# Wide output projection, sample rows and first index key in column tiles, first loads in places of their own

## The chip, the cores and the metric

The kernel runs on one core of a Trainium2 chip. The metric is the time of one execution on the device in microseconds (us); lower is better. Five engines work side by side, each through its own instructions in a fixed order: PE (TensorE, matmuls; its weight loads are a row of their own, PEld), DVE (VectorE), ACT (ScalarE), POOL (GpSimd) and SP (SyncE, which issues the DMAs).

## The reference

One inference step of a layer with three groups of attention heads, for 512 prompt rows and 32 sample rows that continue a cache of 1024 rows. D is 1024; all arrays are fp32.

```python
def layer(x, ...):                      # prompt: 512 rows; sample: 32 rows with caches
    z = rmsnorm(x, norm_mix_g) @ w_in   # 1024 -> 13 column groups
    qa, ka, va, ga, qb, kb, vb, gb, qm, gm, qi, ki, wi = split(z)
    # A, 6 heads x 64: own chunk of 64 rows and 8 chunks before it, relative-position bias
    # B, 6 heads x 64: an indexer (8 heads x 32, ONE shared key ki of 32 columns) scores all
    #    earlier rows; attention only over the best 128 (prompt) or 256 (sample)
    # M, 4 heads x 64: attention to 256 memory rows, mk, mv = rmsnorm(mem) @ w_mem_kv
    mix = concat(A(...) * silu(ga), B(...) * silu(gb), M(...) * silu(gm))   # rows x 1024
    return rmsnorm(x + mix @ w_out, norm_out_g)
```

The outputs are y for prompt and sample, and the new keys, values and index keys.

## The kernel before, in words

**Arithmetic.** A product in fp32 accuracy is made of three fast matmuls in the type fp32r: each operand is split in a high part and a low remainder, and h·wh, l·wh and h·wl are summed in PSUM (`tokens`, `group_t`, `out_part`). So each chunk of weights goes through a chain: `w_load` (SP) brings `raw`, `rounded` (ACT) makes `wh`, and a subtraction (`w_split`) makes `wl`, on POOL, or on DVE for the chunks named in `WV`. The input goes the same way: ACT makes `xTh`, DVE `xTl` (512 prompt columns and 32 sample columns); `xF` is the sample part in plain fp32, made on POOL.

**Sample rows.** The 32 sample rows would fill a quarter of PE's 128 columns. In the input projections they are therefore done in plain fp32 with the unsplit `raw`, as four matmuls side by side in four tiles of 32 columns (`divided`), each with a quarter of the contraction. Elsewhere they are not in four tiles: in the attention of the sample (`sample`, with mix 0 for A, 1 for B and 2 for M) the value blocks stand still (64 columns, two tiles) and the 32 probabilities of a head move (`mix_of`); in the output projection the sample is a fifth tile of rows, `oS`, with its high and low parts as 64 columns.

**Order.** No engine decides at run time what comes next. A planner (`Line`) runs while the program is built: it keeps a clock for each engine, adds for each operation a modelled duration (`cost`), for DVE and POOL a rule on the memory port that they share (`port`), and lets generators (tasks) issue their operations when the modelled clocks say that inputs are there (`at`, `sure`). What comes out is one static list for each engine. PE's list is filled by the projections; pieces of attention are put between them when they are ready in the model. So a change in any number of the model moves operations everywhere.

**Stages on PE.** The string `START` orders the first loads. The first projection is the index one (`index_group`), by chunks of two rows of blocks, with 296 columns for tiles 1 to 3 and only the 32 key columns for tile 0. Then come the groups of `EARLY` (`ka`, `va`, `mk`, `mv`, then the transposed ones `qa`, `ga`, `qm`, `gm`) and of `LATE` (`gb0`, `kb`, `qb`, `vb`, `gb1`, `gb2`). A's and M's attention units (`attend`) are woven in from the moment that their inputs exist, then B's. The output projection has two parts in `out_part`: first the heads of A and M, in four column blocks of 256, which fills PE beside B's last units, then, when all units are done, the heads of B in two blocks of 512, each as two accumulations of 256 columns. `residual` (DVE) adds the products to x in `xr`, and `settle` makes the last norm with the running sum `ss`: ACT squares, DVE adds, POOL takes the root (`ALU.pow`), DVE and ACT scale, SP stores.

In the profile all recorded operations carry one line, L273, the call inside the planner's wrapper (L288 after the change), so instructions are told apart by tiles. `bank` is a PSUM bank, `xT` the normed and transposed input, `k`, `q` keys and queries of a unit, `z` and `pt` probabilities and their transposes, `oA`, `oB`, `oM` the gated results by group, with h and l for the parts.

Of the kernel before, what the change touches and what calls it, by code (L numbers as in the profile page):

```python
# [17 lines left out]
P = 128  # L18
# [16 lines left out]
WV = (0, 2)  # L35
# [7 lines left out]
EARLY = ("ka", "va", "mk", "mv", "qa0", "qa1", "qa2", "ga0", "ga1", "ga2", "qm0", "qm1", "gm0", "gm1")  # L43
# [3 lines left out]
class Line:  # L47
# [4 lines left out]
    def __init__(self):  # L52
        self.clk = dict.fromkeys(("PE", "DVE", "ACT", "POOL", "SP", "DMA"), 0.0)
        self.ready, self.used = {}, {}
        self.boxes = {}
        self.tables = {"exp": (AF.Exp, AF.Tanh)}
        self.table = None
        self.mode = None
        self.taken = []
        self.tasks = []  # L60
        self.seq = 0
        self.margin = 0.3
        self.time = 0.0
        self.window, self.busy, self.slow = 0.0, 0.0, True
        self.warm = None

    def cost(self, eng, op, outs, ins, kw):
        if eng == "PE":
# [12 lines left out]
            if mode != self.mode:  # L81
                self.mode = mode
                d += 0.095 + (0.104 if fast else 0.056) * mode[1] / P
            return d
# [6 lines left out]
        if eng == "ACT":  # L91
# [5 lines left out]
            return t  # L97
        return 0.15 + n * (0.0034 if op == "tensor_scalar" else 0.0021)
# [204 lines left out]
def hybrid_step(ctx: ExitStack, tc: tile.TileContext, a: dict):  # L303
# [80 lines left out]
    oS = cp.tile([P, 8, 2 * T], F32R, name="oS")  # L384
    m8 = cp.tile([P, 8], F32, name="m8")

    rs, r16, ss = (cp.tile([P, 8], F32, name=n) for n in ("rs", "r16", "ss"))
# [56 lines left out]

    w_in, w_out, w_mem = a["w_in"], a["w_out"], a["w_mem_kv"]
    NATURAL = {"i": (QI, 296), "ka": (KA, 384), "va": (VA, 384), "kb": (KB, 384), "qb": (QB, 384), "vb": (VB, 384)}
    TURNED = {"qa": QA, "ga": GA, "qm": QM, "gm": GM, "gb": GB}
    for nm in ("i",) + EARLY + LATE:
# [4 lines left out]
        elif nm in ("mk", "mv"):  # L453
            c0 = 256 * (nm == "mv")
            w_cols(w_mem, c0, c0 + 256)
# [14 lines left out]
    met = []  # L470
    allowed = [0]

    def w_load():
        party = {p + j for _, p, _ in parties for j in range(NK // 2)}
        for i, (w, k, nk, lo, hi) in enumerate(w_list):
            yield from line.wait(lambda: allowed[0] > i and (i < 8 or len(split) > i - 4 and (i - 4 not in party or i - 4 in met)))
# [5 lines left out]
            else:  # L482
                yield wp.free("raw")
                raw = wp.tile([P, nk, hi - lo], F32, tag="raw", name="raw", bufs=4)
# [3 lines left out]
    def w_split():  # L488
        at = {}
        for i in range(len(w_list)):  # L490
            far = i >= n_in + 3 and i % 2
            yield from line.wait(lambda: len(raws) > i and (not far or wq))
            pw, n = (rp, 4) if i < 4 else (wq[0], 2) if far else (wp, 3)
            mine = at.setdefault(n, [])
            yield from line.wait(lambda: len(mine) < n or used["done"] > mine[-n])
            mine.append(i)
            raw = raws[i]
            yield max(line.at(raw), pw.free("wl"))
            wh = pw.tile(list(raw.shape), F32R, tag="wh", name="wh", bufs=n)
            wl = pw.tile(list(raw.shape), F32R, tag="wl", name="wl", bufs=n)  # L500
# [56 lines left out]
    def tokens(acc, xh, xl, w, c, t, c0, c1, first, last):  # L557
# [3 lines left out]
        for kk in range(2):  # L561
            k = 2 * c + kk
# [4 lines left out]
            PE.matmul(o, h, wl[:, kk, c0:c1], start=False, stop=last and kk == 1)  # L567

    def needs_of(xh, xl, w, c, t):
        k = slice(2 * c % 4, 2 * c % 4 + 2)  # L570
        return w + tuple(x[c // 2][:, k, t * P:(t + 1) * P] for x in (xh, xl))
# [11 lines left out]
    def group_n(xh, xl, n, tiles, done, then, r0, there):  # L583
# [3 lines left out]
        for c in range(NK // 2):  # L587
            w = w_next()
            line.until(lambda: there[0] > c)
            for t in range(tiles):  # L590
                yield needs_of(xh, xl, w, c, t) + ((acc[t],) if c == 0 else ())
                tokens(acc[t], xh, xl, w, c, t, 0, n, c == 0, c == NK // 2 - 1)
                made[0] += c == NK // 2 - 1
# [32 lines left out]
    mTl = [cp.tile([P, 4, NM], F32R, tag=n, name="mTl") for n in ("kb", "gate1")]  # L626
# [3 lines left out]
    def x_load():  # L630
        c = len(x_raw)
        yield from line.wait(lambda: x_done[0] > c - 3)
        t = rp.tile([P, 2, N], F32, tag="xr", name="xr", bufs=3)
# [5 lines left out]
    def m_load():  # L639
# [3 lines left out]
        m_raw.append(t)  # L643

# [41 lines left out]
    def norms():  # L686
        for i in range(NT + 1 + NM // P):
# [7 lines left out]
            G.tensor_scalar(ss[:n, i:i + 1], ss[:n, i:i + 1], EPS, None, op0=ALU.add)  # L695
            G.tensor_tensor(rs[:n, i:i + 1], ss[:n, i:i + 1], nhalf[:n], op=ALU.pow)
            G.tensor_scalar(r16[:n, i:i + 1], rs[:n, i:i + 1], 1.0 / 16, None, op0=ALU.mult)
# [40 lines left out]
    def start():  # L738
# [12 lines left out]
        DMA.dma_start(gT[1], a["norm_mem_g"])  # L751
# [11 lines left out]
    def load_tables(d):  # L763
# [5 lines left out]
        def scale():  # L769
            for t in range(NT):  # L770
# [23 lines left out]

    rot, wI = ix.tile([P, NT, 9, 32], F32, name="rot"), ix.tile([P, NT, 8], F32, name="wI")
# [3 lines left out]
    def i_done(t, acc):  # L799
# [4 lines left out]
        if t > 0:  # L804
            A.copy(wI[:, t, :], acc[:, 288:296])
# [5 lines left out]
        if t > 0:  # L811
            for r in (rs, r16):
                G.tensor_scalar(wI[:, t, :], wI[:, t, :], r[:, t:t + 1], None, op0=ALU.mult)
        indexed.append(t)

    def index_group():
        acc = take(NT)
        for c in range(NK // 2):
            w = w_next()
            line.until(lambda: x_done[0] > c)  # L820
            for t in (1, 2, 3, 0):
                yield needs_of(xTh, xTl, w, c, t)
                tokens(acc[t], xTh, xTl, w, c, t, *((256, 288) if t == 0 else (0, 296)), c == 0, c == NK // 2 - 1)
                if c == NK // 2 - 1:
                    line.spawn(i_done(t, acc[t]))

# [173 lines left out]
    bi = {n: cp.tile([P, 1], I32, name="bi_" + n) for n in ("thr0", "thr1", "flip", "neg", "ok", "dig", "next")}  # L1000
    bf = {n: cp.tile([P, 1], F32, name="bf_" + n) for n in ("sum", "t", "c", "m", "need", "try", "min")}
# [142 lines left out]
    def memory(nm, dst, out):  # L1144
        def done(t, acc):
            scaled(dst[:, t, :], acc[:, 0:256], rs[:, NT + 1 + t:NT + 2 + t])

        def finish():
            store_rows(a[out], dst)
            over[nm] = True  # L1150

        return group_n(mTh, mTl, 256, NM // P, done, finish, NT + 1, m_done)
# [3 lines left out]
    def projections(order):  # L1156
        nonlocal ka, va
        for nm in order:
# [15 lines left out]
            elif nm[0] == "m":  # L1174
                line.run(memory(nm, mk if nm == "mk" else mv, f"new_mem_{nm[1]}_p"))
# [10 lines left out]
    def sample(mix, nh, nb, kt, cv, qT, kn, vn, pts, zin):  # L1186
# [17 lines left out]
        o_ps = bank()  # L1204
        for g0 in range(0, nh, 4):
            hs = list(range(g0, min(g0 + 4, nh)))
            rows = T * len(hs)
            z = zin(g0, rows)
# [39 lines left out]
            for k0 in range(0, nk, 512):  # L1248
# [16 lines left out]
                blocks += [(pt, b, i, w) for b, i, w in bw]  # L1265
            yield line.sure(*(x[0] for x in blocks))
            yield line.sure(*cv)

            def mix_of():
                for j0 in range(0, len(hs), 2):  # L1270
                    for pt, b, i, w in blocks:
                        for j in (j0, j0 + 1):
                            h = hs[j]
                            e = h % 2
                            vv = cv[b // 4][:, b % 4, h * 64:h * 64 + 64] if b < nb else vn[:, h * 64:h * 64 + 64]
# [510 lines left out]
```

## Time and profile before

| what | value |
| --- | --- |
| time, median of 3 runs | 363.25 us (363.15 to 365.74) |
| profiled execution, time | 362.68 us |
| profiled execution, span of its instructions | 360.6 us |
| mean granted TensorE clock | 0.996 |
| instructions | 7941 |
| PE busy | 350.7 us in 2961 matmul records |
| DVE, ACT, POOL busy | 276.6, 219.6, 191.0 us |
| DMA | 46.35 MB, mean 129 GB/s |

The span runs from the first to the last instruction; the time has 2.1 us more around it. A row of the timeline has start, duration, engine, line, operation, output<-inputs, partitions x elements, and in brackets how long the engine had been idle and who released it. Matmuls overlap, so their durations (0.28 to 0.34 us) are not what one costs; the distance from start to start is. An fp32 matmul leaves two records, an fp32r one leaves one.

### The profile page before, as it was taken

To read this page: it belongs to the slowest core of one execution; us is meant where nothing else is said; L and a number is where in the kernel's file an instruction comes from. 1 tells how busy PE (TensorE), PEld (TensorE's weight loads), DVE (VectorE), ACT (ScalarE), POOL (GpSimd) and SP (SyncE) were. 2 spreads that over 40 slices of the span, in tenths; PEclk is the share of its full clock that TensorE was granted. 3 is DMA by queue.
4 is the path that set the end of the run, shared out by engine and by line. 5 is a ranking of instruction groups with operands and counts; after the bars stand their busy time and mean duration, and the time that the engine had idled before them with its cause. 6 is when DMAs were issued, how large, how long until landed. Compare 5 with 4: busy or idle time off the path is not lost.

```text
span 360.6 us, 7941 instructions
## 1 busy us (share of the span) xinstructions
PE 350.7 (97%) x2961; PEld 320.0 (89%) x2961; DVE 276.6 (77%) x696; ACT 219.6 (61%) x521; POOL 191.0 (53%) x213
## 2 busy tenths in 40 slices
PE   8999999999999999999999999999999999999991
PEld 8989988999998989898699898999979878888991
DVE  3665977797888978888999885999868576866463
ACT  5856767896747775595856553217665665544443
POOL 1778983375465574148436464534597412140751
PEclk9999999999999999999999999999999999999998
DMA  7998351475493322531203250133489412000015
GB/s 251 362 362 264 97 176 58 126 202 147 119 293 119 88 52 62 182 90 44 90 3 87 88 166 20 51 108 115 128 294 362 133 45 104 2 2 2 0 40 209
DMA packets 41478, 46.35 MB, mean 129 GB/s; under 512 B 5184, under 2 KB 36544, under 8 KB 41440
## 3 DMA queue, kind: packets, MB, share of 16 engines
q1 hardware_dynamic: 41440, 45.85, 39.9%
q8 instruction: 23, 0.38, 0.4%
q14 instruction: 15, 0.12, 0.1%
HBM read 39.67 MB, written 6.16 MB: 127 GB/s over the span
## 4 chain that ended last, share of the span: by engine, by line
PE 89%; DVE 4%; DMA 2%; issue 1%; ACT 1%; POOL 1%; SPq 1%; POOLq 0%; ACTq 0%; DVEq 0%
PE bank L273 89%; DMA raw<-in_w_in_dram 2%; POOL ss L273 1%; DVE ysel L273 1%; ACT sq L273 1%; DVE xr L273 1%; SPq L273 1%; DVE z L273 1%; DVE m L273 0%; DVE xTl L273 0%; DVE gate L273 0%; ACT wh L273 0%; ACT xTh L273 0%; DVE o L273 0%; DVE pt L273 0%
## 5 line engine op out<-in xcount | busy, mean ns | idle before, releaser
L273 POOL TENSOR_TENSOR wl<-raw,wh 128x512 fp32r<-128x512 f32 (+2 forms) x68 | 110.0, 1622 | 78.2 <-ACT wh L273 74.4
L273 ACT ACTIVATE wh<-raw 128x512 fp32r<-128x512 f32 (+2 forms) x70 | 50.1, 719 | 33.1 <-issue 13.6
L273 PE MATMUL bank<-wh,xTh 128*128 128x384 f32 (+1 forms) x192 | 65.3, 340 | 0.0
L273 PE MATMUL bank<-wl,xTh 128*128 128x384 f32 (+1 forms) x192 | 63.3, 330 | 0.0
L273 PE MATMUL bank<-wh,xTl 128*128 128x384 f32 (+1 forms) x192 | 63.2, 329 | 0.1
L273 ACT ACTIVATE z<-z,st 128x256 f32<-128x256 f32 (+3 forms) x77 | 41.0, 550 | 21.0 <-DVE st L273 20.9
L273 PE MATMUL bank<-xTh,wh 128*128 128x272 f32 x208 | 46.3, 304 | 0.0
L273 PE MATMUL bank<-xTh,wl 128*128 128x272 f32 x208 | 43.0, 288 | 0.0
L273 PE MATMUL bank<-xTl,wh 128*128 128x272 f32 x208 | 43.0, 288 | 0.0
L273 PEld LDWEIGHTS bank<-wh,xTh 128*128 128x128 f32 x192 | 36.1, 188 | 2.3 <-issue 1.6
L273 PEld LDWEIGHTS bank<-wh,xTl 128*128 128x128 f32 x192 | 36.2, 189 | 0.4 <-DVE xTl L273 0.3
L273 PEld LDWEIGHTS bank<-wl,xTh 128*128 128x128 f32 x192 | 36.1, 188 | 0.2 <-POOL wl L273 0.2
L273 PEld LDWEIGHTS bank<-xTh,wh 128*128 128x128 f32 x208 | 32.7, 189 | 1.7 <-issue 0.8
L273 PEld LDWEIGHTS bank<-xTh,wl 128*128 128x128 f32 x208 | 32.6, 189 | 0.1
L273 PEld LDWEIGHTS bank<-xTl,wh 128*128 128x128 f32 x208 | 32.6, 188 | 0.0
L273 DVE MAX8 m<-ysel 128x8 f32<-128x256 f32 (+2 forms) x48 | 26.4, 549 | 0.0
L273 DVE MATCH_REPLACE8 ysel<-m,ysel 128x256 f32<-128x256 f32 (+2 forms) x48 | 26.1, 543 | 0.0
L273 PE MATMUL bank<-ident,z 128*128 128x128 f32 (+1 forms) x161 | 25.0, 273 | 0.0
L273 ACT COPY pt<-bank 128x512 f32<-128x512 f32 (+1 forms) x26 | 14.1, 543 | 14.3 <-PE bank L273 14.2
L273 DVE SCALAR_TENSOR_TENSOR ysel<-r,wI,ysel 128x256 f32<-128x256 f32 (+2 forms) x21 | 17.8, 849 | 6.0 <-ACT r L273 5.6
L273 POOL TENSOR_TENSOR oBl<-o,oBh 128x128 fp32r<-128x128 f32 (+1 forms) x9 | 4.9, 549 | 30.4 <-ACT oBh L273 30.4
L273 PEld LDWEIGHTS bank<-ident,z 128*128 128x128 f32 (+1 forms) x161 | 18.2, 140 | 2.5 <-issue 1.0
(307 smaller groups left out, 892.6 us busy)
## 6 DMA issues: line engine op xcount, KB each, us to landing
raw<-in_w_in_dram SPq DMA_DIRECT2D x20, 384.0 KB, 3.6
raw<-in_w_in_dram SPq DMA_DIRECT2D x26, 256.0 KB, 2.9
raw<-in_w_out_dram SPq DMA_DIRECT2D x8, 384.0 KB, 3.1
nat<-in_x_prompt_dram SPq DMA_DIRECT2D x4, 512.0 KB, 7.9
raw<-in_w_mem_kv_dram SPq DMA_DIRECT2D x8, 256.0 KB, 2.8
xr<-in_x_prompt_dram SPq DMA_DIRECT2D x4, 512.0 KB, 4.8
out_dram<-xr SPq DMA_DIRECT2D x4, 512.0 KB, 2.6
xr<-in_x_t_dram SPq DMA_DIRECT2D x3, 544.0 KB, 5.8
```

The costliest lines, as they stand in the source:

```text
L273: return fn(*args, **kw)
```

## The change

The output projection is now 512 columns wide. `w_out` comes in 16 chunks of one block of rows by 512 columns instead of 12 chunks (256 columns, two or three blocks). Blocks 0, 1, 2 and 6 (`AM`) make the first part, and 7, 3, 4, 5 (`B`) the second, so one of M's two blocks moves to the second part. Four of these chunks get places of their own in tiles that are free by then. The memory's keys and values become one group `mkv` of 512 columns in 8 chunks. The 512-column groups run with one block of rows per chunk.

```diff
-    for c0 in range(0, D, 256):
-        w_cols(w_out, c0, c0 + 256, 3, 0, 3)
-        w_cols(w_out, c0, c0 + 256, 2, 6, 8)
-    for c0 in range(0, D, 256):
-        w_cols(w_out, c0, c0 + 256, 3, 3, 6)
+    AM, B = (0, 1, 2, 6), (7, 3, 4, 5)
+    for ks in (AM, B):
+        for c0 in range(0, D, 512):
+            for k in ks:
+                w_cols(w_out, c0, c0 + 512, 1, k, k + 1)
...
-    def out_part(parts, c0, n, done, order, apart=()):
+    def out_part(ks, c0, done, order, apart=()):
...
+            n = 512 // halves
+            for f0 in range(0, 512, n):
+                acc, = take(1)
+                o = acc[:, 0:n]
+                for i, k in enumerate(ks):
...
+                    PE.matmul(o, h, wh, start=st, stop=False)
+                    PE.matmul(o, l, wh, start=False, stop=False)
+                    PE.matmul(o, h, wl, start=False, stop=en)
```

The sample leaves `out_part`. `oS` is now one fp32 tile, and `out_sample` multiplies it with the unsplit `raw` in four tiles of 32 columns, one block of rows in each; `out_rows` adds the four results to the sample's x, one after the other on DVE.

```diff
+    def out_sample():
...
+                for j, p in enumerate(ps):
+                    for q, kt in enumerate(B if at_ == 8 else AM):
+                        PE.matmul(p[q * T:(q + 1) * T, :], oS[:, kt, :], raws[i0 + 4 * j + q][:, 0, :],
+                                  start=True, stop=True, tile_position=(0, q * T))
...
+    def out_rows(xrS, ps, rows):
+            for q in range(4):
+                V.tensor_tensor(x, p[q * T:(q + 1) * T, :], x, op=ALU.add)
```

In the sample's attention the probabilities now stand still (32 columns, four tiles, one head in each) and the 64 value columns move. The result comes out as rows, so it is copied into `z`, turned by one PE transpose per group of heads and gated by two DVE operations per group.

```diff
-                            PE.matmul(o_ps[64 * e:64 * e + 64, (h // 2) * T:(h // 2 + 1) * T], vv,
-                                      pt[:, i * rows + T * j:i * rows + T * j + T], start=(b == 0),
-                                      stop=(b * P + w == nk), tile_position=(0, 64 * e))
+                        PE.matmul(o_ps[r * T:(r + 1) * T, g0 * 32 + c:g0 * 32 + c + 64],
+                                  pt[:, i * rows + T * j:i * rows + T * j + T], vv, start=(b == 0),
+                                  stop=(b * P + w == nk), tile_position=(0, r * T))
```

The index key of tile 0 is made apart: `key_weights` multiplies the key's raw weights with the norm's gain on POOL (`gw`, four operations of 128x64), `key0` makes 8 fp32 matmuls of 128 columns in four tiles, and one matmul with a stacked identity sums the four.

```diff
-            for t in (1, 2, 3, 0):
+            for t in range(1, NT):
                 yield needs_of(xTh, xTl, w, c, t)
-                tokens(acc[t], xTh, xTl, w, c, t, *((256, 288) if t == 0 else (0, 296)), c == 0, c == NK // 2 - 1)
+                tokens(acc[t], xTh, xTl, w, c, t, 0, 296, c == 0, c == NK // 2 - 1)
...
+                    PE.matmul(p[q * 32:(q + 1) * 32, 0:P], gw[:, k, :], x_raw[k // 2][:, k % 2, 0:P],
+                              start=(j == 0), stop=(j == 1), tile_position=(0, q * 32))
...
+        PE.matmul(acc[:, 256:288], k4, ident4, start=True, stop=True)
```

At the start, the fourth load of x has a place of its own and waits for none before it; `WV` grows from (0, 2) to (0, 1, 2, 3), so the first four `wl` are made on DVE; the sum of squares gets its epsilon on DVE and one factor `r16` is folded away. In the planner, `cost` has new numbers (among them one for a short matmul before a long one) and `port` a new rule: DVE yields only to a POOL operation that stands first, and an operation of DVE pushes POOL's clock.

```diff
-WV = (0, 2)
+WV = (0, 1, 2, 3)
...
         for s, end, by in self.taken:
-            if by != eng and s <= t < end:
+            if by != eng and s <= t < end and (eng == "POOL" or t > self.kept + 0.02):
                 t = end
+                if eng == "DVE":
+                    break
+        if eng == "DVE":
+            if self.clk["POOL"] > t:
+                self.clk["POOL"] += d
+            self.kept = t + d
```

In `settle` the middle sums go to POOL, and the last half-row scaling of tile 3, not of tile 2, is on DVE.

```diff
-            V.tensor_scalar(run, new, EPS if j == 0 else old, None, op0=ALU.add)
+            if j == 0:
+                V.tensor_scalar(run, new, EPS, None, op0=ALU.add)
+            else:
+                G.tensor_tensor(run, new, old, op=ALU.add)
...
-        if t == NT - 2:
+        if t == NT - 1:
             V.tensor_scalar(y[:rows, 0:512], y[:rows, 0:512], run, None, op0=ALU.mult)
         else:
             A.activation(y[:rows, 0:512], y[:rows, 0:512], AF.Copy, scale=run)
```

What this does to the order stands at three places. The first is the end of the index projection on PE. Before, the tail of each chunk is tile 0's narrow matmuls:

```order
L273 MATMUL bank<-wh,xTh_83 128x32
L273 MATMUL bank<-wh,xTl_85 128x32
L273 MATMUL bank<-wl,xTh_83 128x32
L273 MATMUL bank<-wh,xTh_83 128x296
L273 MATMUL bank<-wh,xTl_85 128x296
L273 MATMUL bank<-wl,xTh_83 128x296
```

Now, at the end of the last chunk, PE's list reads as follows; `xr,gw` is the key of tile 0, between the sample's part of the index projection and its part of `ka`:

```order
L288 MATMUL bank<-wh,xTh_82 128x296
L288 MATMUL bank<-wh,xTl_84 128x296
L288 MATMUL bank<-wl,xTh_82 128x296
L288 MATMUL bank<-raw,xF 32x296 x8
L288 MATMUL bank<-xr,gw 32x128 x8
L288 MATMUL bank<-raw,xF 32x384 x8
L288 MATMUL bank<-wh,xTh_81 128x384
```

The 24 narrow matmuls are gone from the chunks, and eight in four tiles stand behind all of them.

The second place is PE's list where B's attention units begin (`k,q` and its two corrections `k,ql` and `kl,q` are a unit's scores). Before, the last projection is done when they start, and the output projection (`oA`) is what fills PE behind them:

```order
L273 MATMUL bank<-k,q 128x128 [waits PE_49]
L273 MATMUL bank<-k,q 128x128 [waits DVE_49]
L273 MATMUL bank<-k,ql 128x128 x2
L273 MATMUL bank<-kl,q 128x128 [waits DVE_49]
L273 MATMUL bank<-kl,q 128x128
L273 MATMUL bank<-k,q 128x256 x2
L273 MATMUL bank<-k,ql 128x256 x2
L273 MATMUL bank<-kl,q 128x256 x2
L273 MATMUL bank<-wh,oAh 128x256
```

After the change, projections of 272 columns (`xT,wh`) stand behind the first scores:

```order
L288 MATMUL bank<-k,q 128x128 [waits DVE_49]
L288 MATMUL bank<-k,q 128x128 [waits Activation_49]
L288 MATMUL bank<-k,ql 128x128 x2
L288 MATMUL bank<-kl,q 128x128 x2
L288 MATMUL bank<-k,q 128x256 x2
L288 MATMUL bank<-k,ql 128x256 x2
L288 MATMUL bank<-kl,q 128x256 x2
L288 MATMUL bank<-xTh_81,wh 128x272 x2
L288 MATMUL bank<-xTl_83,wh 128x272 x2
L288 MATMUL bank<-xTh_81,wl 128x272 x2
```

B's units have moved ahead in the order relative to the projections: 84 projection matmuls of 272 columns follow B's first scores, where there was none.

The third place is the end of DVE's list, tile 2 and tile 3 of the last norm (`xr_3719` and `xr_3720` before, `xr_3765` and `xr_3766` after). Before:

```order
L273 TENSOR_TENSOR xr_3720<-bank,xr_3720 128x256 [waits PE_49] x2
L273 SCALAR_TENSOR_TENSOR xr_3719<-xr_3719,ss,gf 128x512 [waits Activation_49,Pool_49]
L273 TENSOR_SCALAR xr_3719<-xr_3719,ss 128x512
L273 TENSOR_SCALAR ss<-ss 128x1 [waits Activation_49]
L273 SCALAR_TENSOR_TENSOR xr_3720<-xr_3720,ss,gf 128x512 [waits Activation_49,Pool_49]
```

After:

```order
L288 TENSOR_TENSOR xr_3766<-bank,xr_3766 128x256 [waits PE_49] x2
L288 SCALAR_TENSOR_TENSOR xr_3765<-xr_3765,ss,gf 128x512 [waits Activation_49,Pool_49]
L288 SCALAR_TENSOR_TENSOR xr_3766<-xr_3766,ss,gf 128x512 [waits Activation_49,Pool_49]
L288 TENSOR_SCALAR xr_3766<-xr_3766,ss 128x512
```

The sum `ss` of tile 3 no longer stands behind tile 2's two scalings, and the scaling of half a row has moved from tile 2 to tile 3.

More of the change, by code (lines that the diff above doesn't have):

```diff
@@ L57, in __init__ @@
         self.table = None
-        self.mode = None
-        self.taken = []
+        self.mode, self.short = None, False
+        self.taken, self.kept = [], -1.0
         self.tasks = []
@@ L83, in cost @@
                 d += 0.095 + (0.104 if fast else 0.056) * mode[1] / P
+            elif self.short and fast and op != "transpose" and mode == (P, P):
+                d += 0.084
+            self.short = n <= 64 or op == "transpose" and not fast
             return d
@@ L560, in tokens @@
         o = acc[:, c0:c1]
-        for kk in range(2):
-            k = 2 * c + kk
+        nk = wh.shape[1]
+        for kk in range(nk):
+            k = nk * c + kk
             h = xh[k // 4][:, k % 4, t * P:(t + 1) * P]
@@ L581, in evict, with group_n @@
             then()
-    def group_n(xh, xl, n, tiles, done, then, r0, there):
+    def group_n(xh, xl, n, tiles, done, then, r0, there, nk=2):
         acc = take(tiles)
@@ L769, in scale @@
         def scale():
+            yield from line.wait(lambda: count["scored"] > 1)
             for t in range(NT):
@@ L1207, in sample @@
             rows = T * len(hs)
+            if mix == 1 and g0:
+                over["first"] = True
             z = zin(g0, rows)
@@ new lines, in sample @@
+            yield from divided(0, mix_of)
+            yield line.at(o_ps) - 0.1
+            n = T * half
+            for e in range(2):
+                either(z[n * e:n * (e + 1), 64 * e:64 * e + 64], o_ps[n * e:n * (e + 1), g0 * 32 + 64 * e:g0 * 32 + 64 * e + 64])
+            yield line.sure(z)
+            yield from room()
+            p = bank()
+            PE.transpose(p[:, 0:rows], z[0:rows, 0:P], ident[0:rows, 0:rows])
+            yield from line.wait(lambda: mix in gated)
+            yield line.at(p, gates[mix]) - 0.2
@@ L1300, in load_cache, with issue @@
         return out
+    ready, xrS = [], []
+    def out_sample():
+        yield from line.wait(lambda: count["done"] >= n_am and 2 in over)
+        yield cp.free("q2")
+        x = cp.tile([T, D], F32, tag="q2", name="xrS")
+        xrS.append(x)
+        DMA.dma_start(x, a["x_sample"])
+        for need, at_, rows in (((0, 2), 0, (0,)), ((0, 2), 4, (512,)), ((1, 2), 8, (0, 512))):
+            i0 = n_in + at_
+            k = 4 * len(rows)
+            yield from line.wait(lambda: len(raws) >= i0 + k and all(m in over for m in need))
+            yield line.sure(oS, *raws[i0:i0 + k])
+            def issue():
+                ps = [bank() for _ in rows]
+                for j, p in enumerate(ps):
+                    for q, kt in enumerate(B if at_ == 8 else AM):
+                        PE.matmul(p[q * T:(q + 1) * T, :], oS[:, kt, :], raws[i0 + 4 * j + q][:, 0, :],
+                                  start=True, stop=True, tile_position=(0, q * T))
+                return ps
+            ps = yield from divided(len(rows), issue)
+            met.extend(range(i0, i0 + k))
+            line.spawn(out_rows(x, ps, rows))
+    def out_rows(xrS, ps, rows):
+        for p, c0 in zip(ps, rows):
+            x = xrS[:, c0:c0 + 512]
+            for q in range(4):
+                yield max(line.at(p, x) - 0.2, line.idle(V))
+                V.tensor_tensor(x, p[q * T:(q + 1) * T, :], x, op=ALU.add)
+            give(p)
+        if len(rows) > 1:
+            yield from line.wait(lambda: ready)
+            for c0 in rows:
+                yield from settle(NT, c0, 512)
     def sample_a():
```

247 lines of the change are left out of this document (152 added, 95 removed).

## The prediction

> **What bounds the kernel now.** I first read the page's row of busy time and shares of the span:
>
> ```profile
> PE 350.7 (97%) x2961; PEld 320.0 (89%) x2961; DVE 276.6 (77%) x696; ACT 219.6 (61%) x521; POOL 191.0 (53%) x213
> ```
>
> PE is busy for 350.7 of 360.6 us. Then the chain that ended last, in order of time (start, duration, work):
>
> ```profile
> 11.58 154.84 PE bank L273 x1233
> ...
> 179.65 84.66 PE bank L273 x627
> ...
> 265.03 81.72 PE bank L273 x839
> ...
> 356.17 0.75 DVE xr L273
> ```
>
> From 11.58 us on the chain is PE's stream, with a gap of 13 us of other work between 166 and 180, and a tail on DVE. So a matmul taken out of PE's list gives its distance to the next start, as long as weights and attention inputs keep up. How close the others are, the windows show (window, then busy time of PE, PEld, DVE, ACT, POOL, clock, DMA share):
>
> ```profile
> 0.00:20.50 20.50, 19.09 (x133) 18.64 (x133) 11.15 (x13) 12.59 (x18) 10.96 (x18) 1.00 0.93 318
> 180.00:265.00 85.00, 84.66 (x635) 77.95 (x632) 73.48 (x154) 42.04 (x102) 44.71 (x37) 1.00 0.30 92
> 265.00:335.00 70.00, 69.97 (x742) 61.50 (x743) 48.65 (x144) 40.02 (x106) 27.34 (x29) 1.00 0.31 109
> ```
>
> The DMA engines are the second bound at the start (0.93), DVE in the picks of B (73.48 of 85 us); behind 265 us nothing is close to PE.
>
> **The change part by part**, against the profiled execution (362.68 us). That lies 0.57 below the median of the runs, so a median of the change may stand as much above my sum.
>
> *Sample rows of the output projection.* Before, 64 matmuls of `oS`:
>
> ```profile
> 327.77 0.49 PE L273 MATMUL bank<-ident,z 128*128 128x128 f32 x3
> 328.01 0.36 PE L273 MATMUL bank<-wh,oS 128*64 128x256 f32 x1
> 328.21 0.28 PE L273 MATMUL bank<-wl,oS 128*64 128x256 f32 x1
> 328.33 0.28 PE L273 MATMUL bank<-wh,oS 128*64 128x256 f32 x1
> 328.80 0.27 PE L273 MATMUL bank<-ident,z 128*128 128x128 f32 x1
> ...
> 333.59 0.33 PE L273 MATMUL bank<-wh,oS 128*64 128x256 f32 x1
> 335.01 0.28 PE L273 MATMUL bank<-wh,oBh 128*128 128x256 f32 x1
> ```
>
> Six take 0.79 us in a short run (0.132 each) and twelve 1.42 in a long one (0.118): 40 x 0.132 + 24 x 0.118 = 8.1 us. The first of a run costs 0.20 instead of 0.12, so an entry costs 0.08. After, 16 fp32 matmuls of 512 columns in four tiles. The same kind is in the input projection of the sample:
>
> ```profile
> 20.48 2.50 PE L273 MATMUL bank<-raw,xF 128*32 128x296 f32 x32
> 22.91 0.44 PE L273 MATMUL bank<-wh,xTh 128*128 128x384 f32 x1
> ```
>
> These are 16 matmuls (two records each), eight of 296 and eight of 384 columns, 2.43 us from start to start: 0.447 ns a column with the entry. 16 x 512 x 0.447 is 3.7, and two more entries at 0.2 make 4.1. The term is **-4.0** (-3.6 to -4.2). What hides the 16 adds of 32x512 on DVE is that DVE has 21 us free between 265 and 335; the last four must not trail, and they stand before the last tiles in DVE's order.
>
> *Mixes of the sample.* 92 matmuls before:
>
> ```profile
> 302.36 1.13 PE L273 MATMUL bank<-ptS,cache 128*64 128x32 f32 x32
> 303.32 0.29 PE L273 MATMUL bank<-keysB,vbS 128*64 128x32 f32 x4
> ...
> 304.59 0.33 PE L273 MATMUL bank<-ident,z 128*128 128x128 f32 x1
> ```
>
> The two rows come twice before the transpose: 72 records, so 36 matmuls, in 2.23 us, 0.062 each in two tiles, though they move only 32 columns. After, 64 of the 92 run in four tiles with 64 columns; no row shows that. By columns it is 64 x 0.447 = 0.029 us; if 0.062 is a floor for each instruction, nothing is gained. I take 0.032, near the only rows in four tiles: 64 x 0.030 = **-1.9** (0 to -2.1). The other 28 stay in two tiles. Five transposes are new: 0.08 each by the row `ident,z` ahead of `oS` (three in 0.24 us) and an entry of 0.08, **+0.8**. The copies into `z` and the gating lie on DVE and ACT, in the time that they have free.
>
> *First index key and start.*
>
> ```profile
> 16.56 0.30 PE L273 MATMUL bank<-wl,xTh 128*128 128x296 f32 x1
> 16.69 0.18 PE L273 MATMUL bank<-wh,xTh 128*128 128x32 f32 x1
> ...
> 17.28 0.38 PE L273 MATMUL bank<-wh,xTh 128*128 128x296 f32 x1
> 17.50 0.30 PE L273 MATMUL bank<-wh,xTl 128*128 128x296 f32 x1
> ```
>
> Six narrow matmuls take 0.59 us, 24 take 2.36; and the 296-column one behind them costs 0.22, against 0.13 in the stream, four times, 0.3. New are 8 x 128 x 0.447 ns = 0.46 and about 0.3 for the sum with its entry. That is -1.9 on PE. What could take it back is the weights' chain:
>
> ```profile
> 8.51 0.79 DVE L273 SCALAR_TENSOR_TENSOR xTl<-xr,g_mix,xTh 128x544 fp32r<-128x544 f32 x1 [1.17 <-ACT xTh L273]
> 14.11 1.67 POOL L273 TENSOR_TENSOR wl<-raw,wh 128x592 fp32r<-128x592 f32 x1 [1.70 <-ACT wh L273]
> 14.71 1.65 DVE L273 SCALAR_TENSOR_TENSOR xTl<-xr,g_mix,xTh 128x544 fp32r<-128x544 f32 x1 [0.27 <-ACT xTh L273]
> ```
>
> The last `wl` of the index group came at 15.78 (14.11 + 1.67), the last `xTl` at 16.36 (14.71 + 1.65), and the last chunk began at 17.28: 0.9 us to spare, and the fourth x load, no longer behind the others, adds to it. I take **-1.9** (-0.5 if the chain limits, -2.9 if the fourth load and the earlier `wl` also shorten waits).
>
> *Memory group.* Widths compared, start to start:
>
> ```profile
> 54.35 0.62 PE L273 MATMUL bank<-KSs,QSs 128*128 128x512 f32 x2
> 54.81 0.34 PE L273 MATMUL bank<-wh,xTh 128*128 128x384 f32 x1
> ...
> 76.94 0.28 PE L273 MATMUL bank<-wh,mTh 128*128 128x256 f32 x1
> 78.37 0.34 PE L273 MATMUL bank<-KS,QS 128*128 128x384 f32 x1
> ...
> 344.76 0.28 PE L273 MATMUL bank<-wl,oBh 128*128 128x256 f32 x1
> 346.12 0.28 PE L273 MATMUL bank<-wl,oBh 128*128 128x256 f32 x1
> ```
>
> 256 columns cost 1.43/12 = 0.119 in the memory stage and 1.36/12 = 0.113 in the output projection; 512 cost 0.46/2 = 0.230. 96 of 0.119 become 48 of 0.230: **-0.4**.
>
> *Wide output projection.* 384 of 256 columns become 180 of 512 and 24 of 256. At 0.113 and 0.230 that is +0.6, at 0.119 and 0.230 it is -1.4; if 512 costs twice 0.113, 0. I take **0**: width saves nothing where 256 already streams.
>
> *More changes of kind.* PE's order has 237 runs of one kind of matmul after 222; without the five transposes, 10 x 0.08 = **+0.8** (0 to +0.8).
>
> The Trainium skill ("TensorEngine Tiling (Array Packing)", Key Properties) states that a change of tiling mode drains the array. The first `oS` row agrees (0.20 against 0.12), and the rule leaves the sum as it is; it speaks against scattered four-tile pieces.
>
> *At nothing.* 16 chunks of `w_out` instead of 12 carry the same bytes and the same elements through ACT and POOL; SP's issues and the loads lie where the DMA share is 0.31. The constants of the norm, `r16` and the small tiles are single short operations on engines with time free; were they on the path, they would cost 0.2 each.
>
> *Tail.*
>
> ```profile
> 352.58 0.28 PE L273 MATMUL bank<-wl,oBh 128*128 128x256 f32 x1
> ...
> 353.86 0.19 ACT L273 ACTIVATION_READ_ACCUMULATOR sq<-xr 128x1 f32 x1
> 353.90 0.75 DVE L273 SCALAR_TENSOR_TENSOR xr<-xr,ss,gf 128x512 f32<-128x512 f32 x1 [0.59 <-POOL ss L273]
> 354.57 0.48 DVE L273 TENSOR_SCALAR xr<-xr,ss 128x512 f32<-128x512 f32 x1
> 354.97 0.21 DVE L273 TENSOR_SCALAR ss<-ss 128x1 f32<-128x1 f32 x1
> 355.32 0.19 POOL L273 TENSOR_TENSOR ss<-ss 128x1 f32<-128x1 f32 x1 [1.45 <-DVE ss L273]
> 355.59 0.55 POOL L273 TENSOR_TENSOR ss<-ss,nhalf 128x1 f32<-128x1 f32 x1
> ```
>
> The sum of squares is there at 354.05, but DVE adds it at 354.97, behind tile 2's scalings. On POOL it goes on at once, 0.9 us plus a handover earlier; against that DVE has both scalings of tile 3 to do at the end, 0.75 + 0.48 where ACT did one beside it. **-0.7** (0 to -1.0).
>
> Sum: -4.0 - 1.9 + 0.8 - 1.9 - 0.4 + 0 + 0.8 - 0.7 = -7.3, so 362.7 - 7.3 = **355.4 us**.
>
> **The rivals.**
>
> *Small prices fail (chance 0.12).* The mixes have a floor per instruction (0), the start gives 0.5, and the width costs 0.6: -4.0 + 0 + 0.8 - 0.5 - 0.4 + 0.6 + 0.8 - 0.7 = -3.4, 359.3 us. For it speaks that 32 moving columns already cost 0.062; against it that 296 columns in four tiles cost 0.13.
>
> *The shared port eats the start (0.12).* `xTl` takes 0.79 alone, and 1.65 while POOL's `wl` runs: it ended 0.6 after POOL did. After the change four `gw` stand on POOL, and four `wl` beside the four `xTl` on DVE. If each `gw` holds up DVE by half a us, the last `wl` comes 2 us late, the spare 0.9 is gone, and the term of the start falls to about -0.5: 356.8. The Trainium skill ("SBUF — State Buffer", Who interferes with whom) has it that DVE with two inputs in SBUF and a reading GpSimd exclude each other. The pair 0.79 and 1.65 agrees, and the chance above is for this rule.
>
> *New waits in the new order (0.12).* Two to five us of PE waiting at places that now have none: 357.4 to 360.4, say 358.5. For it speaks that every place moved; against it that PE in 180 to 335 us is idle for 0.37 us only, under the same kind of planner.
>
> *Slower: B's chain becomes the end (0.09).* A unit of B is a sequence of picks on DVE, scores and transposes on PE, softmax on ACT, and `oB` through ACT and POOL. Before, `oB` of the last unit lets that part start at 335.01, and 17.8 us of it follow to 352.85. After, 84 x 0.230 + 24 x 0.113 = 22.0 us of matmuls wait for B, less three of M's block, so 21.5. The filler ahead of it shrinks: 240 x 0.113 + 40 x 0.132 = 32.4 becomes 96 x 0.230 = 22.1. If B's chain ends no earlier than now, because it hangs on the picks and not on PE, the last matmul ends at 335.0 + 21.5 = 356.5, 3.7 later, and with the tail's 0.7 the time is 365.7. It decides slower from a last `oB` at 332.0 on (352.85 - 21.5 + 0.7). Against it: by the order, 84 projection matmuls of 272 columns stand behind B's first scores, some 84 x 0.120 = 10 us by the columns of the 256 rows, so B begins as much earlier as its filler shrinks; but then the picks on DVE must end 10 us earlier in a stretch where DVE is at 86%.
>
> **How the numbers follow.** The forecast has 0.55. All terms at their best give -11.2 (351.5), all at their worst -2.3 (360.4). The range is **351.5 to 360.0**; outside it lie the slower rival, a part of the new waits and of the small prices. About 1% (3.6 us) is what a measurement of this kernel tells from no change. Faster by more than that (under 359.6) are the forecast, the port and a good half of the other two: 0.80; same 0.11; slower 0.09.
>
> **What would show it.** `raw,oS` as 16 matmuls in about 4.1 us in all; `ptS,cache` at about 0.03 us a matmul; the index stage ending at about 18.5 instead of 20.4; `mTh` of 512 columns at 0.230; `oB` 512 wide at 0.227 to 0.230; the last DVE operation ending 3.6 us behind the last matmul's start instead of 4.3. I would be wrong if PE shows stretches of waiting for `z`, `ysel` or `wl` between 20 and 330 us, or if the last `oBl` comes later than 325 us.

## The result, and the profile after

The changed kernel takes **367.29 us** (median of 18 runs, 364.78 to 369.24) against 363.23 us before (18 runs, 362.58 to 365.74). The ratio is 1.0107, with a 95% interval from 1.0087 to 1.0127: slower by 1.1%, where 355.4 was forecast. The profiled execution took 366.74 us, with a span of 364.8.

The page's first row, the busy time and shares of the engines, and its fourth part, the chain that ended last, by engine:

```profile
span 364.8 us, 7448 instructions
PE 347.9 (95%) x2700; PEld 298.5 (82%) x2700; DVE 286.7 (79%) x714; ACT 218.3 (60%) x523; POOL 183.4 (50%) x207
PE 73%; DVE 18%; ACT 2%; issue 2%; DMA 2%; POOL 1%; SPq 0%; POOLq 0%; DVEq 0%; ACTq 0%
```

PE has less to do, 261 matmul records fewer, but the chain that was almost all PE now runs for 18% over DVE. The windows, to be held beside the three of before:

```profile
0.00:20.50 20.50, 18.75 (x146) 17.34 (x150) 12.46 (x18) 12.63 (x19) 10.19 (x24) 1.00 0.91 288
180.00:265.00 85.00, 83.37 (x627) 76.40 (x626) 73.88 (x151) 40.13 (x100) 43.35 (x36) 1.00 0.28 84
265.00:335.00 70.00, 66.37 (x583) 49.14 (x582) 53.01 (x136) 40.33 (x109) 28.98 (x32) 0.98 0.37 129
```

From 265 to 335 us PE is busy for 66.37 of 70 us, where it had 69.97, and its clock has fallen to 0.98. The waits of the weight loads (us in total, times, longest) say for whom:

```profile
PEld bank L288 <- issue: 22.8, 77, 0.8
PEld bank L288 <- ACT z L288: 4.3, 4, 2.9
PEld bank L288 <- DVE kl L288: 1.9, 1, 1.9
PEld bank L288 <- DVE st L288: 1.8, 4, 0.9
```

These are waits for probabilities `z` and for operands that DVE makes. All rows of that view but "issue" sum to 8.2 us before and 19.3 after. Leaving overlaps aside, the PE row itself waits 2.1 us before and 9.9 after. The largest one in the timeline of PE, and what follows it:

```profile
275.11 0.41 PE L288 MATMUL bank<-xTh,wl 128*128 128x272 f32 x2
278.21 0.66 PE L288 MATMUL bank<-ident,z 128*128 128x128 f32 x4 [2.69 <-ACT z L288]
278.80 0.37 PE L288 MATMUL bank<-ident,qbS 32*128 32x32 f32 x3
279.00 0.35 PE L288 MATMUL bank<-ident,kbS 32*128 32x32 f32 x3
279.29 0.59 PE L288 MATMUL bank<-wh,oAh 128*128 128x512 f32 x1
279.68 0.63 PE L288 MATMUL bank<-wh,oAl 128*128 128x512 f32 x1
280.10 0.63 PE L288 MATMUL bank<-wl,oAh 128*128 128x512 f32 x1
```

PE stands still for 2.69 us, and behind that a matmul of 512 columns takes 0.42 us from start to start (279.68 to 280.10) instead of 0.23. The windows of that place show the reason in the third number from the end, the granted clock:

```profile
278.00:280.00 2.00, 1.79 (x12) 1.49 (x13) 1.97 (x5) 1.61 (x5) 1.42 (x2) 0.89 0.73 193
280.00:282.00 2.00, 2.00 (x7) 1.06 (x6) 1.97 (x4) 1.95 (x8) 1.48 (x3) 0.50 0.85 335
282.00:284.00 2.00, 2.00 (x25) 1.79 (x24) 1.94 (x7) 0.69 (x2) 2.00 (x3) 0.76 0.95 303
```

The clock is at half for some 3.4 us, which loses 2 x (0.11 + 0.50 + 0.24) = 1.7 us. Why `z` is late is read on DVE, with one row of ACT (rows of their timelines ahead of the wait's end):

```profile
241.87 2.19 DVE L288 TENSOR_TENSOR rt<-qbS,sin64S 32x384 f32<-32x384 f32 x1 [0.91 <-POOL qb L288]
...
270.45 0.69 DVE L288 CUSTOM_DVE_ANT_0 z<-bank,ysel 128x512 f32<-128x512 f32 x1
...
273.31 1.78 DVE L288 SCALAR_TENSOR_TENSOR ysS<-rank,ysS 128x1056 f32<-128x1056 f32 x1
274.87 0.19 ACT L288 ACTIVATION_READ_ACCUMULATOR z<-z,st 128x1 f32 x1
275.01 0.67 DVE L288 TENSOR_TENSOR xrS<-bank,xrS 32x512 f32<-32x512 f32 x1
275.61 1.00 DVE L288 COPY pt<-bank 128x384 f32<-128x384 f32 x2
276.64 0.68 DVE L288 TENSOR_TENSOR xrS<-bank,xrS 32x512 f32<-32x512 f32 x1
277.25 0.14 DVE L288 RECIPROCAL st<-st 128x2 f32<-128x2 f32 x1
```

The masked scores of the unit are there at 271.1. ACT, in an order as fixed, has their exponentials and row sums ready at 275.06 (274.87 + 0.19); from then on only the reciprocal is missing, and it comes at 277.25, 2.2 us later. Up to 275.1 DVE is at the end of the sample's ranking (`ysS`), and behind that stand two of the 16 new adds to `xrS` and two copies of `pt`. And DVE came to that place late: from 242 to 277 us the chain runs almost without a break over DVE, which works on the sample's rotation, keys and ranking beside POOL's `wl` (the row at 241.87, on 32 partitions and 384 columns, takes 2.19 us; alone it takes 0.55).

### The profile page after: what moved, and what is told of

It reads as the page before. It is cut to its first block, busy times and chain, and to the rows that moved or that the text cites. A ratio compares the mean times of both kernels' runs of the same rounds, so it can differ in the third digit from the quotient of the medians.

```text
span 364.8 us, 7448 instructions
## 1 busy us (share of the span) xinstructions
PE 347.9 (95%) x2700; PEld 298.5 (82%) x2700; DVE 286.7 (79%) x714; ACT 218.3 (60%) x523; POOL 183.4 (50%) x207
## 4 chain that ended last, share of the span: by engine, by line
PE 73%; DVE 18%; ACT 2%; issue 2%; DMA 2%; POOL 1%; SPq 0%; POOLq 0%; DVEq 0%; ACTq 0%
PE bank L288 73%; DVE z L288 3%; DVE rank L288 2%; DMA xr<-in_x_t_dram 2%; DVE rt L288 1%; DVE junkS L288 1%; DVE ysel L288 1%; DVE KSs L288 1%; DVE ysS L288 1%; DVE qbS L288 1%; DVE m L288 1%; POOL qb L288 1%; DVE mTl L288 1%; DVE zS L288 0%; SPq L288 0%
## 5 line engine op out<-in xcount | busy, mean ns | idle before, releaser
L288 POOL TENSOR_TENSOR wl<-raw,wh 128x512 fp32r<-128x512 f32 (+1 forms) x69 | 104.1, 1520 | 76.7 <-ACT wh L288 69.9
L288 PE MATMUL bank<-wh,xTh 128*128 128x384 f32 (+1 forms) x184 | 63.3, 344 | 0.0
L288 PE MATMUL bank<-wl,xTh 128*128 128x384 f32 (+1 forms) x184 | 61.3, 333 | 0.5 <-POOL wl L288 0.2
L288 ACT ACTIVATE wh<-raw 128x512 fp32r<-128x512 f32 (+2 forms) x73 | 50.0, 691 | 19.3 <-PE bank L288 10.1
L288 PE MATMUL bank<-wh,xTl 128*128 128x384 f32 (+1 forms) x184 | 61.1, 332 | 0.2 <-DVE xTl L288 0.2
L288 ACT ACTIVATE z<-z,st 128x256 f32<-128x256 f32 (+3 forms) x76 | 39.9, 542 | 28.0 <-DVE st L288 28.0
L288 PEld LDWEIGHTS bank<-wh,xTh 128*128 128x128 f32 x184 | 34.6, 188 | 1.7 <-issue 1.2
L288 PEld LDWEIGHTS bank<-wl,xTh 128*128 128x128 f32 x184 | 34.5, 188 | 1.0 <-POOL wl L288 0.6
L288 PEld LDWEIGHTS bank<-wh,xTl 128*128 128x128 f32 x184 | 34.7, 188 | 0.5 <-DVE xTl L288 0.4
L288 ACT ACTIVATE junkS<-ysS,bi 128x1056 int8<-128x1056 f32 x16 | 18.7, 1168 | 4.1 <-DVE bi L288 4.1
L288 ACT ACTIVATE r<-bank 128x512 f32<-128x512 f32 (+3 forms) x30 | 13.9, 482 | 9.4 <-PE bank L288 9.4
```

The lines of the kernel that those rows point to most:

```text
L288: return fn(*args, **kw)
```

## The experiments

**The planner's new numbers, taken back.** The change mixes less work with other planning numbers. Three kernels take the numbers back in the changed one, one puts them into the kernel before.

```diff
 # e1, e3: port() as before
-            if by != eng and s <= t < end and (eng == "POOL" or t > self.kept + 0.02):
+            if by != eng and s <= t < end:
 ...
-        if eng == "DVE":
-            if self.clk["POOL"] > t:
-                self.clk["POOL"] += d
-            self.kept = t + d
 # e2, e3: cost() as before
-            elif self.short and fast and op != "transpose" and mode == (P, P):
-                d += 0.084
 ...
-        if op == "memset":
-            return 0.05 + n / 1000.0
-        if n == 1:
-            return 0.57 if kw.get("op") == ALU.pow else 0.22
```

> The changed kernel with the planner's rule on the shared port as before; the costs and all other parts of the change stay. Theory (the new rule lets DVE run too early in the model, so PE is placed ahead of what DVE delivers): the PE waits at 160-190 and 260-290 us shrink from 8 us to under 3, time 357 to 361. Rival 1 (DVE has 10 us more work, whatever the order): PE waits stay, 365 to 368. Rival 2 (any order that hurries PE runs into the picks and the sample's ranking on DVE): the first row of waits moves to another place, 363 to 368.

> The changed kernel without the planner's new cost numbers (short before long, memset, one column); the port rule and the rest stay. Theory (the port rule is at fault): no gain, 365 to 369. If the cost numbers are at fault: 357 to 361. Rival 2 (DVE in any order): 363 to 368.

> The changed kernel with both of the planner's parts as before, so only the data path of the change is left. Theory: 356 to 361, which would be what the change of the work itself is worth. Rivals 1 and 2: 363 to 368, with PE waiting 6 us or more for DVE and ACT between 160 and 345 us.

> The kernel before with the new port rule and the new costs in its planner, and nothing else of the change. Theory: 4 to 8 us slower than before, 367 to 371. Rivals: within 2 us of before, 361 to 365, since the work on each engine is the same.

| kernel | median, us | ratio to before, 95% interval | clock |
| --- | --- | --- | --- |
| e1, port rule as before | 371.9 | 1.0245 (1.0228 to 1.0262) | 0.983 |
| e2, costs as before | 376.68 | 1.0377 (1.0344 to 1.0411) | 0.969 |
| e3, both as before | 361.51 | 0.9962 (0.9944 to 0.998) | 0.996 |
| e4, before with both new | 373.91 | 1.0285 (1.0259 to 1.0311) | 0.981 |

The clock is that of the profiled execution. e1 and e2 came out above every range given for them, e4 above that of its theory, and e3 half a us above its own (356 to 361). With the same numbers in the planner the new data path is faster: by 1.7 us with the old ones (363.22 to 361.51) and by 6.6 us with the new ones (373.91 to 367.29), each pair being two orders only. But my theory, that the port rule is at fault, falls: taking the rule back alone makes the kernel slower, and so does taking back the costs alone. Four sets of numbers give 361.5, 367.3, 371.9 and 376.7 us for the same operations. In the profiled execution of e2 PE has four waits of 1.6 to 3.3 us, and the clock is at half for 20 us; in e3 it waits twice for more than 1 us behind the start, for 1.45 and 1.72 us, and the clock stays up until PE is done.

**The same kernels, other draws.** If numbers that say little about the chip move the time that much, a number that says nothing should too. `SLACK` multiplies the modelled durations of all engines but PE. It was moved in steps of 0.01 from 1.30, in both kernels.

```diff
-SLACK = 1.3
+SLACK = 1.31      # and 1.28, 1.29, 1.32
```

> The kernel before, with the planner's factor on the durations of DVE, ACT and POOL at 1.31 instead of 1.3. No operation is added or taken away; only the places in the lists move. Theory now (the order is one draw of many and the order of before was a good one): 365 to 375. Rival (orders from a sound model are all about alike, and the new rule and costs spoil the model): 362 to 365.

> As e5_before_131 with the factor at 1.29. Theory: 365 to 375. Rival: 362 to 365.

> The changed kernel with the factor at 1.31. Theory (a draw of many): anywhere from 359 to 375, with PE's waits at other places than 183 and 276 us. Rival (the new rule and costs place PE ahead of DVE in a systematic way): 366 to 369, with waits at the same places.

> The changed kernel with the factor at 1.29. Theory: anywhere from 359 to 375. Rival: 366 to 369.

> The kernel before with the planner's factor at 1.28. Draw of many: 363 to 380, the likeliest 365 to 372, with the granted clock falling where a wait is over 2.5 us. Rival (before is sound at all factors but 1.31): 363 to 365.

> As e13_before_128 with the factor at 1.32; same expectations.

> The changed kernel with the factor at 1.28. Draw of many, about 7 us less work on PE: 358 to 372, and over all orders some 4 to 7 us below those of before. Rival (the new rule and costs are at fault in any order): 366 or more.

> As e15_after_128 with the factor at 1.32; same expectations.

Medians of 2 to 18 runs each (e5, e13, e14 and e15 have 2):

| factor | before, us | changed, us | difference |
| --- | --- | --- | --- |
| 1.28 | 366.74 | 360.68 | -6.1 |
| 1.29 | 364.26 | 361.45 | -2.8 |
| 1.30 (as given) | 363.23 | 367.29 | +4.1 |
| 1.31 | 379.76 | 365.52 | -14.2 |
| 1.32 | 367.35 | 363.27 | -4.1 |
| mean of five | 368.3 | 363.6 | -4.6 |

Both rivals failed: before is not sound at all factors but 1.31, and the new rule does not spoil every order. The theory of many draws missed twice itself: e5 is above its range of 365 to 375, and e6 below it, where the rival had it. Nor did all waits move: in e7 PE waits 1.75 us for `z` at 277.84, near the place of the given order. Of five orders, the given one of before is its best, and the given one of the changed kernel is its worst. At each of the other factors the changed kernel is faster. The mean of the differences hangs on 1.31: without it it is -2.2. The slowest order, e5, shows the pattern at its largest (the waits of PE, then two windows of 2 us):

```profile
PE bank L273 <- DVE ql L273: 4.8, 1, 4.8
PE bank L273 <- DVE z L273: 3.4, 1, 3.4
```

```profile
272.00:274.00 2.00, 2.00 (x18) 1.67 (x16) 2.00 (x8) 1.78 (x8) 0.00 (x0) 0.50 0.00 0
274.00:276.00 2.00, 2.00 (x14) 1.25 (x11) 1.96 (x9) 1.59 (x5) 0.41 (x1) 0.50 0.31 63
```

Two waits for DVE, 8.2 us together, and the clock at half for 24 us in and behind them (summed over windows of 2 us, 11.9 us lost). This execution took 18.4 us longer than the profiled one of before (381.06 and 362.68). The two sums make 20.1, with some overlap, since clock lost while PE stands still costs nothing.

**One order held, one cause taken away.** In the next four kernels the planner works as in the changed kernel and every list keeps its order; only single operations are issued shorter, in another form or more often.

```diff
 # e9: the eight adds of the sample's first part are planned whole, issued on one column
+            if self.line.narrow:
+                args = tuple(x[:, 0:1] if isinstance(x, bass.AP) else x for x in args)
 ...
+                line.narrow = len(rows) == 1
                 V.tensor_tensor(x, p[q * T:(q + 1) * T, :], x, op=ALU.add)
+                line.narrow = False
 # e10: ahead of the wait at 275.5 us, at the last 272-column matmul of that unit
+            if op == "matmul" and kw.get("stop") and outs[0].tensor.name == "bank_3579":
+                for _ in range(20):
+                    fn(*args, **dict(kw, stop=False))
 # e11: the last six wl of the input weights, planned as before, issued as a fill
+            if self.line.blank:
+                return self.engine.memset(args[0].bitcast(F32), 0.0)
 ...
+            line.blank = n_in - 6 <= i < n_in
             tsub(V if i in WV else G, wl, raw, f(wh))
+            line.blank = False
 # e12: e9 and e11
```

> The changed kernel with every list in its order, but the eight adds of the sample's first part (32x512 on DVE) made on one column, so the sample's y lacks most of that part. Two of them stand on DVE in front of the reciprocal that PE waits for at 275.5 us. Theory (PE waits for DVE's queue there, and the slow clock behind the wait is part of the price): the wait falls from 2.7 to about 1.4 us and the slow stretch is shorter or gone, 363.5 to 366. Rival (DVE's queue is not what ends that wait): 366.5 to 368.

e9: 365.37 us, ratio 1.0043 (1.0027 to 1.006). The same place now reads (the planner's call is on line 290 or 291 in these kernels)

```profile
276.10 0.41 PE L291 MATMUL bank<-xTh,wl 128*128 128x272 f32 x2
278.20 0.66 PE L291 MATMUL bank<-ident,z 128*128 128x128 f32 x4 [1.69 <-ACT z L291]
...
279.60 0.39 PE L291 MATMUL bank<-wh,oAl 128*128 128x512 f32 x1
279.83 0.39 PE L291 MATMUL bank<-wl,oAh 128*128 128x512 f32 x1
```

The wait is 1.69 us instead of 2.69, and the 512-column matmul behind it takes 0.23 us: the clock did not fall in this execution. This execution ran 1 us late from before 184 us on (the wait that ends at 183.12 in the changed kernel ends at 184.09 here), so `z` came 1 us earlier by its own clock, though at the same 278.20. The gain is 1.0 in the wait and 1.7 in the clock, less that 1 us; the profiled execution took 365.21 us, 1.5 less, and the median fell by 1.9. Two of the four runs have a mean clock of 0.986 (365.5 and 365.7 us) against 0.996 in the other two (364.3 and 365.2), so in those it was lower, at a place that no trace shows.

> The changed kernel with every list in its order, but 20 further copies of one 272-column matmul (2.5 us) put into the 2.7 us in which PE waits at 275.5 us; one gate is wrong by them. Nothing is made earlier by it. Theory (an idle PE loses its clock for the next 3.4 us, which costs 1.7 us): the granted clock stays at 1.0 behind the place and the time is 365 to 366. Rival (the low clock has another cause, or costs nothing since DVE is behind anyway): 367 to 368.

e10: 365.41 us, ratio 1.0053 (1.0038 to 1.0068). Nothing was made earlier, PE only kept busy:

```profile
275.21 2.63 PE L290 MATMUL bank<-xTh,wl 128*128 128x272 f32 x20
277.69 0.29 PE L291 MATMUL bank<-xTh,wl 128*128 128x272 f32 x1
278.19 0.66 PE L291 MATMUL bank<-ident,z 128*128 128x128 f32 x4 [0.22 <-ACT z L291]
...
280.37 0.39 PE L291 MATMUL bank<-wh,oAl 128*128 128x512 f32 x1
280.60 0.40 PE L291 MATMUL bank<-wl,oAh 128*128 128x512 f32 x1
```

`z` comes when it came, and the matmuls behind it run at 0.23 us. 20 useless matmuls make the kernel 1.9 us faster. So the pause is what lowers the clock here, and the low clock costs what the windows say. In this execution the clock was at half for 3.4 us at another place, from 176.9 us on, behind pauses of 0.46 and 0.74 us that the changed kernel's execution has as well, without a fall. It cost nothing: PE's wait of 1.61 us for `kl` at 183.12 in the changed kernel is gone in e10, and both stand alike at 275 us.

> The changed kernel with every list in its order, but the last six subtractions for the input weights on POOL (241 to 262 us) replaced by fills of the same tiles, which write and don't read; so the last projections lack a correction term. In the profile DVE loses 6.8 us there to operations that take longer beside POOL. Theory (the collisions make DVE late for the wait at 275.5 us): DVE's excess there falls under 3 us, the wait is gone, 362 to 364.5. Rival (collisions only eat time that DVE has): 366 to 368.

e11: 363.52 us, ratio 1.0 (0.999 to 1.0009), 3.8 us less than the changed kernel. DVE's row of above, and the wait:

```profile
241.97 0.55 DVE L291 TENSOR_TENSOR rt<-qbS,sin64S 32x384 f32<-32x384 f32 x1 [0.91 <-POOL qb L291]
```

```profile
274.55 0.41 PE L291 MATMUL bank<-xTh,wl 128*128 128x272 f32 x2
276.39 0.66 PE L291 MATMUL bank<-ident,z 128*128 128x128 f32 x4 [1.43 <-ACT z L291]
```

Summed over DVE's operations, what they take beyond the shortest of their shape is about 7 us from 240 to 260 us in the changed kernel, about 2 in the one before and under 1 here. With that gone the unit's `z` comes 1.8 us earlier, and the clock stays up in the profiled execution: 1.8 + 1.7 is most of the gain of 3.8. The wait is shorter, not gone as expected; DVE itself waits for PE now, 1.33 and 0.52 us just ahead of that reciprocal. The fills are also shorter than the subtractions (1.42 us for the first two, where those took 3.94), so `wl` came sooner too; e11 does not part this from DVE's gain.

> e9_narrow_adds and e11_no_collision together, every list in its order. Theory: no wait left at 275 us, 361.5 to 364, hardly better than e11_no_collision alone, since only one wait can be taken away there. Rival: 366 to 368.

e12: 363.27 us, ratio 0.9989 (0.998 to 0.9999): 0.25 us less than e11. The wait is 0.90 us, where none was expected. Little was left to gain at that place, as expected.

## Why the prediction was wrong, step by step

**The terms of the work were right.** The last matmuls of the index projection and the key of tile 0, then the mixes of B's first four heads, and the sample's last eight products, on PE:

```profile
18.27 0.29 PE L288 MATMUL bank<-wl,xTh 128*128 128x296 f32 x1
18.50 1.20 PE L288 MATMUL bank<-raw,xF 128*32 128x296 f32 x16
19.52 0.62 PE L288 MATMUL bank<-xr,gw 128*32 128x128 f32 x16
19.95 1.47 PE L288 MATMUL bank<-raw,xF 128*32 128x384 f32 x16
21.36 0.44 PE L288 MATMUL bank<-wh,xTh 128*128 128x384 f32 x1
...
319.39 1.10 PE L288 MATMUL bank<-cache,ptS 128*32 128x64 f32 x64
320.31 0.29 PE L288 MATMUL bank<-vbS,keysB 128*32 128x64 f32 x8
320.54 0.66 PE L288 MATMUL bank<-ident,z 128*128 128x128 f32 x4
...
338.45 1.92 PE L288 MATMUL bank<-raw,oS 128*32 128x512 f32 x16
340.31 0.50 PE L288 MATMUL bank<-whl,oBh 128*128 128x512 f32 x1
```

- *Sample's output projection*, forecast 8.1 to 4.1 us: 1.86 for the last eight (338.45 to 340.31), and 3.8 for all 16 from start to start. Right.
- *Mixes*, forecast 0.062 to 0.032 us: 36 matmuls in 1.15 us (319.39 to 320.54), 0.032. Right. The value had no row before; the price by columns was the right end of the range.
- *First key and start*, forecast -1.9 and an end at about 18.5: the key's eight take 0.43, the stage ends at 18.50, and `ka` begins at 21.36 instead of 22.91, and the sum by the identity, at 27.75, takes 0.14. That is -1.4: inside the range, smaller than forecast, and the port did not eat the start, which was a rival.
- *Widths*: the median distance of a 512-column matmul is 0.232 to 0.235 us, for `mTh` and `oB` alike, against 0.230 forecast. Near.
- *Tail*, forecast 3.6 us from the last matmul's start to DVE's end: 357.75 to 361.23, 3.5. Right:

```profile
357.75 0.28 PE L288 MATMUL bank<-wl,oBh 128*128 128x256 f32 x1
...
360.75 0.48 DVE L288 TENSOR_SCALAR xr<-xr,ss 128x512 f32<-128x512 f32 x1
```

**The step that failed** is the frame of the forecast, set in its first part: that a matmul taken out of PE's list gives its distance, "as long as weights and attention inputs keep up". They did not. To the last matmul's start PE takes 357.75 instead of 352.58 us, 5.2 more. Its own waits are 7.8 more (2.1 to 9.9) and the clock costs 1.7, so what is left of the work is 4.3 less; by the waits of the weight loads (11.1 more) it is 7.6 less. The forecast's -6.6 ahead of the tail lies between the two. By kinds (distances from each matmul to the next, summed over the trace) the projections of the input, without the narrow matmuls that are gone, went from 180.3 to 186.1 us, and the attention (scores, transposes of `z`, products with `pt`) from 55.8 to 58.7: the waits sit in these. Both signs of being wrong that the prediction named came true: PE waits for `z`, and the last `oBl` comes later than 325 us.

Three readings led to it:

- *"What hides the 16 adds of 32x512 on DVE is that DVE has 21 us free between 265 and 335."* The mean does not show it. Two of the adds stood ahead of one reciprocal, and e9 shows 1.9 us for them, with the clock.
- *"New waits in the new order (0.12)"*, two to five us. The mechanism was this one. It was 8 to 11 us by the two rows of waits, and its second part, the clock behind a pause, was not in the sum at all: before shows the clock down only at the very end, when PE is done. That before had 0.37 us of idle PE in 155 us (180 to 335) was put down to its kind of planner. That does not hold: the order at 1.29 has 0.34 too, but those at 1.28, 1.32 and 1.31 have 1.9, 3.2 and 5.4, under the same planner. The given order was a lucky one.
- *"Slower: B's chain becomes the end (0.09)"*, from a last `oB` at 332.0 on. The last `oBl` ended at 332.3 instead of 334.9: B gained 2.6 us, not the 10 of the filler that was gone. It did not become the end, since PE goes from 333.17 to its last matmul without a wait; B cost its time earlier, at 275 us. The doubt put down there, that DVE at 86% would have to deliver 10 us earlier, is what happened: its first masked scores of B come at 262.93 instead of 267.04, 4.1 us earlier.

The range ended at 360.0 because it was made of the terms' bounds, and no term stood for the order. From the forecast to the median it is 11.9 us; the place that e9 to e12 work on accounts for 3.8 of them (e11); the rest no run took apart. Over five orders the change is worth -4.6 us in the mean, against -7.3 forecast; whether the rest is lost in any order of this kind, or by chance in five, these runs do not settle. The profiled executions speak for a lasting part: PE's own waits are 6.7 to 9.9 us in all five orders of the changed kernel, and 2.1 to 6.0 in four of the five of before (12.2 in e5). Why was not taken apart; e11 shows that DVE's collisions with POOL are part of it in one order.

**A version that beats both**: the changed kernel with the factor at 1.28 takes 360.68 us (two runs), 0.9924 of before (0.9896 to 0.9953).

## What to carry to other kernels

When a static order decides, the time of one kernel is one draw: compare two versions over several orders (here a factor moved by 1% did it) before a change is called good or bad, and before a wait-free profile is taken as a property of the design. A change that makes the bound engine faster asks the next one to deliver earlier; look for single operations ahead of what is waited for, not for the mean of free time. A pause of the TensorE can be paid twice, once as the pause and once as the half clock behind it.

## What the runs showed of the hardware

A pause of 2.69 us set the granted clock to 0.50 for about 3.4 us, and in other orders pauses set it so for one or several such stretches: the losses come in steps of 1.7 us (1.7 in the changed kernel, 5.1 in e1 and e4, 10.2 in e2). The length of a pause alone does not decide. In e7 one of 1.39 us was enough, while pauses of 1.4 to 1.8 us in e3, e9, e11 and elsewhere in e7 passed in the profiled executions:

```profile
167.46 0.40 PE L288 MATMUL bank<-xTh,wh 128*128 128x272 f32 x1 [1.39 <-DVE gate L288]
```

```profile
168.00:170.00 2.00, 2.00 (x15) 0.74 (x18) 1.96 (x5) 2.00 (x5) 0.65 (x2) 0.58 0.00 0
```

In the clock records of all 18 traces the changes lie on a grid of 3.413 us, at another phase in each execution. Counted on that grid (by the modelled ends of the matmuls), every stretch at full clock with 1.8 us or more of idle PE was followed by half clock, and none with less than 1.1; in between both occurred (1.39 us in e7 and in e14 with, 1.61 in the changed kernel and 1.69 in e9 without). The Trainium skill ("TensorE: Matmul & The Clock Gate", Part 1: The HAM clock gate) states a free-running window of some 3.4 us, and half the rate after a window that was idle; the step of 1.7 us agrees with the window, but here a pause of 2.69 us, shorter than it, was enough (e10 and e9 against the changed kernel).

The spread between executions fits a phase that differs, though only one execution of each kernel was traced. In the 18 runs of the changed kernel the three with a clock of 0.994 took 364.8 to 365.5 us, the five at 0.991 or 0.992 took 366.7 to 367.4, and the ten at 0.983 to 0.987 took 366.5 to 369.2, for one and the same list of instructions. In e3 the two runs at 0.989 and 0.991 took 362.9 and 363.0 us, the four at 0.994 or 0.996 took 361.0 to 361.6.

A DVE operation with two inputs in SBUF that took 2.19 us beside POOL's subtraction took 0.55 beside a fill of the same tile, which only writes; that is what the Trainium skill ("SBUF — State Buffer", Who interferes with whom) states.
